# Issuing one pair's far-value loads behind the next pair's first query copies, in a hybrid decoder layer

## The chip, the cores and the metric

The kernel runs on one core of one Trainium2 chip. The metric is device time in microseconds (us) of one execution. The engines are TensorE (PE in the profile, with its weight loads as PEld), VectorE (DVE), ScalarE (ACT), GpSimd (POOL) and SyncE (SP), which here issues the DMAs (SPq in the profile).

## The reference

One decoder layer over 1024 tokens of width 1024. Two mixers share one input projection: an attention with 8 heads of 64 columns, and a gated recurrence with 4 heads of 128. Their outputs are joined and projected, then a squared-ReLU feed-forward of width 4096 follows; each part has an RMS norm ahead of it and one behind it. The change touches the attention alone:

```python
DILATED_PATTERNS = ((128, 1), (512, 4), (2048, 16))
...
def dilated_mixture_attention(q, k, v, slopes):
    outs, lses = [], []
    for window, dilation in DILATED_PATTERNS:
        o, lse = dilated_branch(q, k, v, slopes, window, dilation)
        outs.append(o)
        lses.append(lse)
    w = jax.nn.softmax(jnp.stack(lses, axis=0), axis=0)
    o = jnp.sum(w[..., None] * jnp.stack(outs, axis=0), axis=0)
    return o.astype(q.dtype)
```

Each pattern lets a query see keys at a stride (every key of the last 128, every 4th of the last 512, every 16th of all), with a bias that falls with the distance. Mixing the three by their denominators is the same as one softmax over the joint keys, with a bias table that counts how many patterns reach a key.

## The kernel before

**Numbers in two parts.** Every product is made in float32 by splitting each operand into a rounded part (names ending in h, or hi) and the rest (l, lo) and multiplying the parts (`three_pass`, lines 90 to 92: three matmuls).

**Stages.** The input is normed and turned, the recurrence's four heads run first (`hgrn_core`), and the attention's projections are laid between their steps. The attention then runs head by head, in four pairs of two heads; output projection and feed-forward follow.

**How the order is set.** The program is written out by hand. Projections are generators that hand out PE work in small pieces; `fill` takes pieces from them between the steps of the recurrence and of the attention, by estimated costs. Each engine works through its own list in program order, and so does SP: a DMA whose data are not ready, or whose target is still read, holds up all DMAs behind it. `attn_proj(pr)` projects pair `pr`: queries (`pm_aq`, in two halves of 512 tokens), values (`pm_av`) and keys (`pm_ak`). Pairs 0 and 1 are projected during the last recurrence head.

**Queries.** For each half, `qf` is written from PSUM by DVE (L793), ACT rounds it to `hiq` and POOL subtracts (`both_parts`, L719 and L720). Both tiles come from a pool of just two buffers with the tag "half", which the next half uses again. Four DMAs then copy the parts to the stacked query tiles `q` of the pair's two heads (L798 and L799). Those stacks come from the tag "S", whose nine buffers the recurrence's tiles use too: `q` of the second head of pair 1 takes the one that `at`, the score tile of the last recurrence head, held.

**Keys of pair 0.** `keys_read` writes the two parts of the keys and copies them with eight DMAs for each half (L737, names `hik`/`kf` for the first half and `kp` for the second).

**Values.** `values_turn` transposes the values of 512 tokens, writes them to `v`, and sends the blocks that the far keys need to a DRAM tile `vd` (L767). The far values are the keys beyond the near blocks, taken at stride 4. `far_load(pr)` takes two slabs and reads them back in far order: six DMAs at L672 into `vf`. For pair 0 it is called at the end of the second `values_turn`; for the other pairs from the attention's loop.

**The attention's steps.** For each head there are eight items: diagonal blocks D0 to D3, far F0 and F1, near N0 and N1. `look` multiplies keys and queries into a bank of the tag "s", of which there are two, and DVE adds the bias and takes the minimum (L901, tile `bt` holds the bias). `raise_` is ACT's exponential (L954), `turn` transposes on PE (`pt_D`, L964) and splits the result on ACT and DVE (`pth` L993, `ptl` L994), `weigh` multiplies with the values (`pov`, L1012, and `pov_far` with the far values, L1028). `swap_low` (L935, `px`) is a small product that moves minima between token orders; its bank is one of the two of "s" too. `gated` (L645) ends the last recurrence head on DVE.

Of the kernel before, what the change touches and what calls it, by code (L numbers as in the profile page):

```python
# [9 lines left out]
F32R = mybir.dt.float32r  # L10
# [7 lines left out]
P = 128  # L18
T = 1024
# [9 lines left out]
DIL = 4  # L29
# [3 lines left out]
def f32(ap):  # L33
    return ap.bitcast(F32)
# [3 lines left out]
def hymba_layer(ctx, tc, x, w_in, w_out, w_ff1, w_ff2, g_pre, lb_logits, g_mix, g_post,  # L38
# [13 lines left out]
    def slab(tag, name, dtype=F32, shape=(P, T)):  # L52
        return sp.tile(list(shape), dtype, tag=tag, name=name,
                       bufs={"S": 9, "T": 9, "P": 3, "BT": 2, "V8": 2, "R": 1}[tag])

    def bank(tag, name):
        return ps.tile([P, 512], F32, tag=tag, name=name,
                       bufs={"mm": 2, "s": 2, "t": 2, "pv": 2}[tag])

    def half(name, dtype=F32):  # L60
        return sp.tile([P, 512], dtype, tag="half", name=name, bufs=2)
# [86 lines left out]
    def w_get(i, ahead=1):  # L148
        while done[1] < min(i + 1 + ahead, len(stream)):
            w_split()  # L150
        return parts[i]
# [240 lines left out]
    def proj_t(w, name, hf, out_box):  # L392
        wh, wl = kc(w[0]), kc(w[1])
        pm = bank("mm", f"pm_{name}{hf}")
        for k in range(NK):
            three_pass(pm, (wh[:, k], wl[:, k]), part(hT, k, hf), k == 0, k == NK - 1)
            out_box[0] = pm
            if k < NK - 1:
                yield 650.0


    def in_blocks(ap):
        return ap.rearrange("p (j i r) -> p j r i", i=32, r=DIL)
# [4 lines left out]
    def by_class(ap):  # L408
        return ap.rearrange("p (j r i) -> p j r i", i=32, r=DIL)
# [58 lines left out]
    def rrow_by_class(hf):  # L468
        sl = slice(hf * 512, hf * 512 + 512)
        moved = half(f"rc{hf}")  # L470
        S.activation(moved.rearrange("p (r m) -> p r m", r=DIL), classes(rrow[:, sl]), AF.Copy)
        S.activation(rrow[:, sl], moved, AF.Copy)
# [187 lines left out]
    fars = {}  # L660

    def key_blocks(ap, j0, j1):
        return ap.rearrange("p (r j i) -> p j r i", r=DIL, i=32)[:, j0:j1]

    def far_load(pr):
        fars[pr] = [slab("T", f"vf{pr}_{c}", F32R, (P, DIL, 2, 2, 64)) for c in range(2)]
        v2 = v_dram[pr].rearrange("(two odd) k c -> odd k two c", odd=2)
        for c in range(2):
            for odd in range(2):
                for c_, p0, k0, n in ((0, 0, 64 * odd, P), (1, 0, P - P * odd, 64), (1, 64, P - P * odd, 64)):  # L670
                    if c_ == c:
                        nc.sync.dma_start(out=f32(fars[pr][c][p0:p0 + n]).rearrange(  # L672
                            "p (two odd) h a d -> odd p two (h a d)", odd=2)[odd], in_=v2[odd, k0:k0 + n])
# [42 lines left out]
    def both_parts(full, name, hi=None):  # L716
        eng = G if hi is None else V
        hi = half(f"hi{name}", F32R) if hi is None else hi
        S.activation(hi, f32(full), AF.Copy)  # L719
        eng.tensor_tensor(out=full, in0=f32(full), in1=f32(hi), op=ALU.subtract)  # L720
        return hi, full
# [34 lines left out]
    def values_turn(tag="mm"):  # L756
        pr, vs, full, hf = turn_later.pop(0)
        pt = bank(tag, f"pvt{pr}{hf}")
        for j in range(4):
            TE.transpose(pt[:, j * P:(j + 1) * P], full[:, j * P:(j + 1) * P], ident)  # L760
        ptv = pt.rearrange("p (j h d) -> p j h d", j=4, h=2)
        dst = vs[:, hf * 4:hf * 4 + 4]
        S.activation(dst[:, :, :, 0, :], ptv, AF.Copy)
        V.tensor_tensor(out=dst[:, :, :, 1, :], in0=ptv, in1=f32(dst[:, :, :, 0, :]), op=ALU.subtract)
        b = slice(0, 4) if hf == 0 else slice(4, 6)
        for r in range(DIL):
            nc.sync.dma_start(out=v_dram[pr][r].rearrange("(n i) c -> i n c", i=32)[:, b],  # L767
                              in_=f32(vs[32 * r:32 * r + 32, b]).rearrange("p n h a d -> p n (h a d)"))
        if hf == 1 and pr == 0:
            far_load(0)  # L770

    def attn_proj(pr):
        stacks = [{}, {}]
        box = [None]
        while pr > 1 and not second_done[pr - 2]:
            yield None
        w = w_get(A0 + 3 * pr, 0)
        for hf in range(2):
            sl = slice(hf * 512, hf * 512 + 512)
            for n, cost in enumerate(proj_t(w, f"aq{pr}", hf, box)):  # L780
                if hf == 0 and n == 3 and turn_later:
                    values_turn()
                    cost += 450.0
                if hf == 0 and n == 4:
                    w_get(A0 + 3 * pr)
                if pr == 0 and hf == 0 and n == 5:
                    rrow_by_class(1)
                yield cost
            if hf == 0:
                for i in range(2):  # L790
                    stacks[i]["q"] = slab("S", f"q{pr}_{i}", F32R)
            full = half(f"qf{pr}{hf}", F32R)
            V.tensor_tensor(out=by_class(f32(full)), in0=in_blocks(box[0]),  # L793
                            in1=rrow[:, sl].rearrange("p (r j i) -> p j r i", r=DIL, i=32), op=ALU.mult)
            hi, lo = both_parts(full, f"q{pr}{hf}")
            for i, (a, b) in enumerate(halves):
                c, d = halves[1 - i]
                nc.sync.dma_start(out=f32(stacks[i]["q"][a:b, sl]), in_=f32(hi[a:b]))  # L798
                nc.sync.dma_start(out=f32(stacks[i]["q"][c:d, sl]), in_=f32(lo[a:b]))  # L799
            yield 650.0  # L800
        wv = w_get(A0 + 3 * pr + 1, 0)
        vs = None

        def values(hf):
            for n, cost in enumerate(proj_t(wv, f"av{pr}", hf, box)):
                if n == 4 and (pr > 0 or hf == 0):
                    w_get(A0 + 3 * pr + 1 + hf)
                if pr == 0 and hf == 1 and n == 6:
                    values_turn("s")
                    cost += 450.0  # L810
                yield cost
            full = half(f"vf{pr}{hf}")
            V.tensor_tensor(out=by_class(full), in0=in_blocks(box[0]),
                            in1=rrow[:, hf * 512:hf * 512 + 512].rearrange("p (r j i) -> p j r i", r=DIL, i=32), op=ALU.mult)
            turn_later.append((pr, vs, full, hf))
            yield 650.0

        vs = slab("V8", f"v{pr}", F32R, (P, NT, 2, 2, 64))
        yield from values(0)
        if pr == 0:  # L820
            yield from values(1)
        while pr > 0 and not first_done[pr - 1]:
            yield None
        wk = w_get(A0 + 3 * pr + 2, 0)
        for i in range(2):
            stacks[i]["kh"] = slab("S", f"kh{pr}_{i}", F32R)
            stacks[i]["kl"] = slab("S", f"kl{pr}_{i}", F32R)
        pairs[pr] = (stacks, vs)
        for hf in range(2):
            for n, cost in enumerate(proj_t(wk, f"ak{pr}", hf, box)):  # L830
                if n == (3 if pr else 6) and hf == 0:
                    values_turn("mm" if pr else "s")
                    cost += 450.0
                if pr == 0 and hf == 1 and n == 5:
                    w_get(A0 + 2)
                yield cost
            keys_read(pr, box[0], hf)
            if hf == 0 and pr == AH // 2 - 1:
                early_rows()
            yield 650.0  # L840
        if pr > 0:
            yield from values(1)
# [273 lines left out]
    def early_rows():  # L1116


        early["rows"] = wide.tile([P, NE, AW], F32, tag="A", name="erows")
        early["table"] = wide.tile([P, 2, T], F32, tag="A", name="etable")  # L1120
        early["order"] = early["table"][:, 1, :P]
        G.tensor_copy(early["order"].rearrange("p (i r) -> p i r", r=DIL), ident.rearrange("p (r i) -> p i r", r=DIL))
        early["mt"] = [wide.tile([P, 2, 2, 4, P], F32R, tag="A", name=f"emt{q}") for q in range(NE // 2)]
        for q in range(NE // 2):
            nc.sync.dma_start(out=early["rows"][:, 2 * q:2 * q + 2],
                              in_=mix_dram[2 * q * P:2 * (q + 1) * P, :AW].rearrange("(n p) d -> p n d", p=P))
# [1180 lines left out]
```

## Time and profile before

| what | value |
|---|---|
| three runs | 1196.8, 1198.42, 1199.7 us (median 1198.42) |
| the profiled execution | 1198.21 us |
| its span, first to last instruction | 1196.4 us |
| mean granted TensorE clock | 0.997 |
| PE busy | 1183.7 us (99%) |
| DVE, ACT, POOL busy | 839.9, 548.6, 296.0 us |
| DMA queue that SP feeds | 174.37 MB, 45.2% of 16 engines' span |

The profile is one execution. Busy time of PE is modelled and counts a matmul as busy while it is in the pipeline, so neighbouring rows overlap. A row of a timeline has its start, its length, the engine, the source line, the operation, the tiles (written <- read) and in brackets the idle time of that engine just before it and what ended it. A row of the windows has the stretch, its length, the busy time of PE, PEld, DVE, ACT and POOL with the number of instructions, the granted clock of TensorE (1.00 is full), the share of the DMA engines in use and GB/s. A row of the waits says who waited for whom, the sum in us, how often, and the longest. SPq rows show the time in which SP issues a DMA, not the transfer.

### The profile page before, as it was taken

To read this page: it belongs to the slowest core of one execution; us is meant where nothing else is said; L and a number is where in the kernel's file an instruction comes from. 1 tells how busy PE (TensorE), PEld (TensorE's weight loads), DVE (VectorE), ACT (ScalarE), POOL (GpSimd) and SP (SyncE) were. 2 spreads that over 40 slices of the span, in tenths; PEclk is the share of its full clock that TensorE was granted. 3 is DMA by queue.
4 is the path that set the end of the run, shared out by engine and by line. 5 is a ranking of instruction groups with operands and counts; after the bars stand their busy time and mean duration, and the time that the engine had idled before them with its cause. 6 is when DMAs were issued, how large, how long until landed. Compare 5 with 4: busy or idle time off the path is not lost.

```text
span 1196.4 us, 17598 instructions
## 1 busy us (share of the span) xinstructions
PE 1183.7 (99%) x6486; PEld 1008.3 (84%) x6486; DVE 839.9 (70%) x1427; ACT 548.6 (46%) x1082; POOL 296.0 (25%) x283
## 2 busy tenths in 40 slices
PE   9999999999999999999999999999999999999997
PEld 8898989878888888888888888888888888888886
DVE  5686969586666667675697666766677653578796
ACT  7633424333556667755653222222244544444562
POOL 0121212001111110152512776566540000000022
PEclk9999999999999999999999999999999999999999
DMA  5222323137454555372424565553687434533337
GB/s 219 71 68 85 98 84 110 42 104 188 95 134 104 142 145 143 93 236 91 173 98 159 175 215 208 178 182 143 218 324 271 162 104 143 174 90 104 107 105 281
DMA packets 90549, 175.49 MB, mean 147 GB/s; under 512 B 14944, under 2 KB 42464, under 8 KB 90464
## 3 DMA queue, kind: packets, MB, share of 16 engines
q1 hardware_dynamic: 90320, 174.37, 45.2%
q8 instruction: 51, 0.84, 0.3%
q14 instruction: 34, 0.28, 0.1%
q10 hardware_dynamic: 144, 0.00, 0.0%
HBM read 116.91 MB, written 47.99 MB: 138 GB/s over the span
## 4 chain that ended last, share of the span: by engine, by line
PE 75%; ACT 1%; DMA 1%; DVE 1%; issue 0%; SPq 0%; DVEq 0%; POOLq 0%; POOL 0%; ACTq 0%
PE f L2047 18%; PE f2s L2047 7%; PE pwo L92 2%; PE pwo L90 2%; PE pwo L91 2%; PE pm_ak L90 1%; PE pm_ak L92 1%; PE pm_ak L91 1%; PE pm_aq L90 1%; PE pov L1012 1%; PE pm_aq L92 1%; PE pm_av L90 1%; PE pm_aq L91 1%; PE pm_av L92 1%; PE pm_av L91 1%; PE pt_D L964 1%
## 5 line engine op out<-in xcount | busy, mean ns | idle before, releaser
L87 DVE TENSOR_TENSOR al<-ar,ah 128x1024 fp32r<-128x1024 f32 x56 | 70.7, 1262 | 81.3 <-ACT ah L86 78.9
L2047 PE MATMUL f<-bh,ah 128*128 128x512 f32 x320 | 124.5, 389 | 0.0
L2047 PE MATMUL f<-bl,ah 128*128 128x512 f32 x320 | 124.5, 389 | 0.0
L2047 PE MATMUL f<-bh,al 128*128 128x512 f32 x320 | 124.5, 389 | 0.0
L86 ACT ACTIVATE ah<-ar 128x1024 fp32r<-128x1024 f32 x56 | 59.2, 1056 | 85.8 <-DMA ar<-actd 84.0
L2047 PEld LDWEIGHTS f<-bh,ah 128*128 128x128 f32 x320 | 60.1, 188 | 12.6
L2047 PEld LDWEIGHTS f<-bl,ah 128*128 128x128 f32 x320 | 60.1, 188 | 12.5
L2047 PEld LDWEIGHTS f<-bh,al 128*128 128x128 f32 x320 | 60.1, 188 | 12.3
L2121 POOL TENSOR_SCALAR lbl<-ssq 128x1 f32<-128x1 f32 x4 | 4.1, 1013 | 244.1 <-ACT fd L2117 243.8
L1670 POOL TENSOR_TENSOR e<-x,e 128x512 f32<-128x512 f32 x14 | 21.6, 1540 | 131.9 <-DVE x L1621 124.7
L2047 PE MATMUL f2s<-bh,al 128*128 128x512 f32 (+1 forms) x128 | 48.9, 382 | 0.0
L2047 PE MATMUL f2s<-bl,ah 128*128 128x512 f32 (+1 forms) x128 | 48.9, 382 | 0.0
L2047 PE MATMUL f2s<-bh,ah 128*128 128x512 f32 (+1 forms) x128 | 48.9, 382 | 0.0
L703 POOL TENSOR_SCALAR tout<-traw 128x256 f32<-128x256 f32 x16 | 18.3, 1146 | 101.0 <-DMA traw<-in_bias_tab_dram 101.0
L87 DVE TENSOR_TENSOR bl<-br,bh 128x1024 fp32r<-128x1024 f32 x32 | 40.2, 1255 | 0.8 <-ACT bh L86 0.7
L2064 ACT ACTIVATE acc<-f 128x512 f32<-128x512 f32 x28 | 16.7, 598 | 49.2 <-PE f L2047 49.2
L751 POOL TENSOR_TENSOR kl<-kf,kh 64x512 fp32r<-64x512 f32 x12 | 16.2, 1350 | 79.2 <-ACT kh L750 79.2
L86 ACT ACTIVATE bh<-br 128x1024 fp32r<-128x1024 f32 x32 | 33.6, 1051 | 3.4 <-PE f L2047 2.3
L87 DVE TENSOR_TENSOR wl<-raw,wh 128x1024 fp32r<-128x1024 f32 x21 | 25.7, 1225 | 9.9 <-ACT wh L86 9.9
L90 PE MATMUL pwo<-woh,mt 128*128 128x512 f32 x80 | 32.2, 403 | 0.0
L92 PE MATMUL pwo<-woh,mt 128*128 128x512 f32 x80 | 31.3, 391 | 0.0
L91 PE MATMUL pwo<-wol,mt 128*128 128x512 f32 x80 | 31.2, 390 | 0.0
(1723 smaller groups left out, 3899.0 us busy)
## 6 DMA issues: line engine op xcount, KB each, us to landing
ar<-actd SPq DMA_DIRECT2D x56, 512.0 KB, 3.6
br<-in_w_ff_dram SPq DMA_DIRECT2D x16, 1024.0 KB, 5.9
raw<-in_w_in_dram SPq DMA_DIRECT2D x28, 512.0 KB, 3.9
w1r<-in_w_ff_dram SPq DMA_DIRECT2D x14, 1024.0 KB, 6.4
actd<-e SPq DMA_DIRECT2D x17, 768.0 KB, 4.2
actd<-e SPq DMA_DIRECT2D x11, 1024.0 KB, 4.1
xr<-in_x_dram SPq DMA_DIRECT2D x8, 512.0 KB, 8.1
raw<-in_w_out_dram SPq DMA_DIRECT2D x8, 512.0 KB, 3.9
```

The source lines that it names most:

```text
L86: S.activation(hi, src, AF.Copy)
L87: eng.tensor_tensor(out=lo, in0=src, in1=f32(hi), op=ALU.subtract)
L90: TE.matmul(dst, lhs[0], rhs[0], start=start, stop=False)
L91: TE.matmul(dst, lhs[0], rhs[1], start=False, stop=False)
L92: TE.matmul(dst, lhs[1], rhs[0], start=False, stop=stop)
L703: G.tensor_scalar(by_class(dst[:, part_ * w:(part_ + 1) * w]), in_blocks(raw[:, FAR * DIL:]), 8.0, None, op0=ALU.mult)
L751: G.tensor_tensor(out=kl[a:b], in0=src, in1=f32(kh[a:b]), op=ALU.subtract)
L964: TE.transpose(pt[:, j * P:(j + 1) * P], st["D"][b][:, j * P:(j + 1) * P], ident)
L1012: TE.matmul(po[:, c0:256], v_of(vs, j), pt[q][:, j, c0:], start=j == 0 and q == 0, stop=j == nj - 1 and q == 1)
L1670: eng[0].tensor_tensor(out=e1[:, 3], in0=a21, in1=e1[:, 2], op=ALU.add)
L2047: TE.matmul(pm, a[:, j, c], b[:, j, d], start=start and j == 0 and q == 0, stop=stop and j == 1 and q == 2, skip_group_check=True)
L2064: S.activation(acc_at(p, i), pm, AF.Copy)
```

## The change

`far_load` is cut in two: `far_room` takes the slabs, `far_load` issues the six DMAs and takes the slabs only where that has not been done. For pair 0 the slabs are taken where they were, at the end of the second `values_turn`; the DMAs are issued in `attn_proj(1)`, behind the four copies of its first query half. The other pairs are as before.

```diff
+    def far_room(pr):
+        fars[pr] = [slab("T", f"vf{pr}_{c}", F32R, (P, DIL, 2, 2, 64)) for c in range(2)]
+
     def far_load(pr):
-        fars[pr] = [slab("T", f"vf{pr}_{c}", F32R, (P, DIL, 2, 2, 64)) for c in range(2)]
+        if pr not in fars:
+            far_room(pr)
...
         if hf == 1 and pr == 0:
-            far_load(0)
+            far_room(0)
...
                 nc.sync.dma_start(out=f32(stacks[i]["q"][c:d, sl]), in_=f32(lo[a:b]))
+            if pr == 1 and hf == 0:
+                far_load(0)
             yield 650.0
```

PE, DVE, ACT and POOL have the same instructions in the same order in both kernels; only SP's list changes. Its first place is behind the copies of pair 0's values to DRAM (`vd`): `vf` are the far values, `kh`, `kl` the stacked keys, `hik`, `kf` and `kp` their sources, `raw` a block of weights. Before:

```order
L767 DMA vd_634<-v_2880 32x4x256 x4
L767 DMA vd_634<-v_2880 32x2x256 x4
L672 DMA vf_0_3065<-vd_634 128x2x256 x2
L672 DMA vf_1_3066<-vd_634 64x2x256 x4
L737 DMA kh_0_3001<-hik_3078 64x4x128 x2
L737 DMA kh_1_3003<-hik_3078 64x4x128 x2
L737 DMA kl_0_3002<-kf_3076 64x4x128 x2
L737 DMA kl_1_3004<-kf_3076 64x4x128 x2
```

At the same place now:

```order
L771 DMA vd_634<-v_2880 32x4x256 x4
L771 DMA vd_634<-v_2880 32x2x256 x4
L741 DMA kh_0_3001<-hik_3072 64x4x128 x2
L741 DMA kh_1_3003<-hik_3072 64x4x128 x2
L741 DMA kl_0_3002<-kf_3070 64x4x128 x2
L741 DMA kl_1_3004<-kf_3070 64x4x128 x2
L107 DMA raw_3128<-in_w_in_dram 128x1024
```

The two groups of `vf` (six DMAs) are gone from here, and the keys follow the values directly. The second place is ten rows on, at pair 1's query copies: `q_0` and `q_1` are the stacks of its two heads, `hiq` and `qf` the two parts, `bt` the bias table of head 1. Before:

```order
L107 DMA raw_3187<-in_w_in_dram 128x1024
L798 DMA q_0_3215<-hiq_3219 64x512
L799 DMA q_0_3215<-qf_3217 64x512
L798 DMA q_1_3216<-hiq_3219 64x512
L799 DMA q_1_3216<-qf_3217 64x512
L855 DMA bt_3263<-tabd_639 128x704
L798 DMA q_0_3215<-hiq_3327 64x512
```

At the same place now:

```order
L107 DMA raw_3181<-in_w_in_dram 128x1024
L802 DMA q_0_3209<-hiq_3213 64x512
L803 DMA q_0_3209<-qf_3211 64x512
L802 DMA q_1_3210<-hiq_3213 64x512
L803 DMA q_1_3210<-qf_3211 64x512
L676 DMA vf_0_3065<-vd_634 128x2x256 x2
L676 DMA vf_1_3066<-vd_634 64x2x256 x4
L861 DMA bt_3263<-tabd_639 128x704
L802 DMA q_0_3209<-hiq_3327 64x512
```

The far loads now stand between the last copy of the first query half and the bias table; the copies of the second query half (`hiq_3327`) come behind both. Line numbers of the changed kernel are 4 to 6 higher here.

## The prediction

> **What bounds the kernel now.** I read the page first, then the waits of TensorE (PE), then the timelines of PE, VectorE (DVE), ScalarE (ACT) and the DMA queue (SPq) around the only place where PE stops for long, and last the windows of that place for the granted clock. The page:
>
> ```profile
> span 1196.4 us, 17598 instructions
> PE 1183.7 (99%) x6486; PEld 1008.3 (84%) x6486; DVE 839.9 (70%) x1427; ACT 548.6 (46%) x1082; POOL 296.0 (25%) x283
> ```
>
> PE is busy 1183.7 of 1196.4 us. A change that leaves PE's work alone can only give back idle PE time or a lowered clock. The longest waits of PE in the whole span (us in total, times, longest):
>
> ```profile
> PE ps_F L896 <- DVE stat L901: 1.7, 1, 1.7
> PE ps_D L896 <- DVE stat L901: 0.7, 1, 0.7
> PE px L935 <- DVE stat L901: 0.5, 1, 0.5
> ```
>
> The first and third lie at one place. PE's timeline there (start, us, what, then the idle time before it):
>
> ```profile
> 299.35 0.39 PE L92 MATMUL pm_av<-hTh,wl 128*128 128x512 f32 x1
> 300.19 0.38 PE L935 MATMUL px<-pick,swap 128*128 128x4 f32 x2 [0.45 <-DVE stat L901]
> 302.23 0.53 PE L896 MATMUL ps_F<-kh,qc 128*128 128x192 f32 x1 [1.66 <-DVE stat L901]
> ...
> 305.11 0.41 PE L1012 MATMUL pov<-pth,v 128*128 128x256 f32 x1
> ```
>
> So 0.45 + 1.66 = 2.11 us are idle. The windows of the next microseconds show a second loss (the number after POOL's is PEclk, the granted clock):
>
> ```profile
> 302.00:303.00 1.00, 0.77 (x4) 0.78 (x4) 0.69 (x4) 0.00 (x0) 0.00 (x0) 0.57 0.28 66
> 303.00:304.00 1.00, 1.00 (x6) 1.00 (x6) 0.57 (x4) 0.00 (x0) 0.00 (x0) 0.50 0.88 199
> 304.00:305.00 1.00, 1.00 (x4) 0.81 (x3) 0.84 (x5) 0.49 (x1) 0.00 (x0) 0.50 0.57 133
> 305.00:306.00 1.00, 1.00 (x6) 0.87 (x6) 0.67 (x3) 0.00 (x0) 0.00 (x0) 0.73 0.00 0
> ```
>
> Right behind the stop the clock is half, for about 3.4 us. What is lost is 0.43 + 0.50 + 0.50 + 0.27 = 1.70 us. One stop thus costs 2.11 + 1.70 = 3.81 us, 0.3% of the span. Who makes PE wait is in DVE's and ACT's timelines:
>
> ```profile
> 296.90 0.60 DVE L645 SCALAR_TENSOR_TENSOR gate<-po,hrs,gate 128x128 f32<-128x128 f32 x2
> 298.83 0.69 DVE L793 TENSOR_TENSOR qf<-pm_aq,rrow 128x512 f32<-128x512 f32 x1 [1.33 <-DMA q<-hiq]
> 299.44 0.68 DVE L901 CUSTOM_DVE_ANT_0 pd<-ps_D,bt 128x512 f32<-128x512 f32 x1
> 300.05 0.08 DVE L901 DVE_READ_ACCUMULATOR2_ANT stat<- 128x1 f32 x1
> 301.13 0.42 DVE L994 TENSOR_TENSOR ptl<-pt_D,pth 128x256 fp32r<-128x256 f32 x1 [1.00 <-ACT pth L993]
> ...
> 302.09 0.08 DVE L901 DVE_READ_ACCUMULATOR2_ANT stat<- 128x1 f32 x1
> ```
>
> ```profile
> 287.00 0.63 ACT L719 ACTIVATE hiq<-qf 128x512 fp32r<-128x512 f32 x1 [5.41 <-DMA kl<-kf]
> ...
> 299.61 0.63 ACT L719 ACTIVATE hiq<-qf 128x512 fp32r<-128x512 f32 x1 [4.11 <-DVE qf L793]
> ...
> 300.74 0.36 ACT L993 ACTIVATE pth<-pt_D 128x256 fp32r<-128x256 f32 x1
> ```
>
> DVE is free at 296.90 + 0.60 = 297.50, but the second pair's second query half (qf, L793) overwrites one of only two "half" buffers, and a DMA still reads that buffer until the copies q<-hiq of the first query half have landed. Everything behind it in DVE's order stands still: the look at ps_D (L901) that frees the bank px needs, and, by way of ACT (hiq, an exponential, then pth) and ptl, the look at ps_F that ends at 302.17 and lets PE go on at 302.23. Those copies are late because of SP's queue:
>
> ```profile
> 275.31 4.44 SPq L672 DMA_DIRECT2D vf<-vd  x6
> ...
> 292.39 0.48 SPq L798 DMA_DIRECT2D q<-hiq  x1
> 292.96 0.55 SPq L799 DMA_DIRECT2D q<-qf  x1
> 293.60 0.55 SPq L798 DMA_DIRECT2D q<-hiq  x1
> 294.20 0.63 SPq L799 DMA_DIRECT2D q<-qf  x1
> ...
> 300.26 0.46 SPq L798 DMA_DIRECT2D q<-hiq  x1
> ```
>
> From 275.31 to 294.83 SP issues almost without a pause, the six far loads first. The chain of waits shows the copy that ends last:
>
> ```profile
> 293.60 5.11 DMA q<-hiq
> ```
>
> 293.60 + 5.11 = 298.71, and DVE starts at 298.83.
>
> **The change part by part.** Nothing is added or removed. PE, DVE, ACT and POOL keep their order; the six far loads go from ahead of the first pair's key copies to behind the four copies of the second pair's first query half, ahead of the bias table bt. The room is still taken at the old place, so no buffer changes.
>
> What comes earlier: the sixteen key copies and two weight loads (raw) in between, by the 4.44 us of the far loads at most. SP would reach the first q<-hiq at 292.39 - 4.44 = 287.95. Its data come from these two rows, the second of them on GpSimd (POOL):
>
> ```profile
> 285.84 0.69 DVE L793 TENSOR_TENSOR qf<-pm_aq,rrow 128x512 f32<-128x512 f32 x1 [0.15 <-PE pm_aq L92]
> 287.76 1.29 POOL L720 TENSOR_TENSOR qf<-qf,hiq 128x512 fp32r<-128x512 f32 x1 [11.68 <-ACT hiq L719]
> ```
>
> The qf waits for PE and does not move. ACT's hiq at 287.00 waited for the key copies; it can now start at 286.53, so hiq is ready near 287.2 and POOL's part near 288.6. The third copy has a wait of its own. The tile q of the second head takes the buffer of the recurrence's score tile `at`, which this last pair of L629 matmuls still reads:
>
> ```profile
> 290.56 0.39 PE L629 MATMUL po<-inat,at 128*128 128x128 f32 x2
> ```
>
> It ends at about 290.95, so this copy goes out near 291.0, not at 293.60 - 4.44 = 289.16: it gains 2.6 us, not 4.4, and SP waits here with the far loads queued behind. With 5.11 us to landing, its own row of before, it lands at 296.1. That is 1.4 us before DVE is free at 297.50. So qf starts at 297.50, 298.83 - 297.50 = **1.33 us** earlier. The fourth copy goes out near 291.6 and lands near 296.7, before ACT needs its buffer for hiq at 299.61 - 1.33 = 298.28.
>
> What is late next: the chain behind qf is unchanged, so ps_F starts at 302.23 - 1.33 = 300.90. The ps_D look ends at 300.13 - 1.33 = 298.80, before PE gets to px, so px's wait of 0.45 goes, and of the 2.11 idle 0.78 stay, all in front of ps_F.
>
> The clock: idle 0.78 where it was 2.11. The nearest row on the other side is the 0.7 us wait of ps_D in the list of PE's waits; it lies in this window, whose clock is 1.00:
>
> ```profile
> 453.00:454.00 1.00, 0.26 (x2) 0.16 (x2) 1.00 (x4) 0.65 (x2) 0.00 (x0) 1.00 0.73 164
> ```
>
> I take the row it is nearest to: no drop, **1.70 us**. The bounds are 0 (it drops all the same) and 1.70. The Trainium skill (TensorE: Matmul & The Clock Gate, Part 1) puts the fall to half clock behind at least one idle window of about 3.4 us that runs free of the program. Here 2.11 us of idling, broken by px, were enough, so the measurement decides against the full idle window; the 3.4 us at half clock agree with the window's length. By the page's rule alone the clock term would not hang on this stop and the sum would be 1.33.
>
> What moves later: the far loads go out from about 292.2 to 292.2 + 4.44 = 296.7. Their first use (all of the kernel's far products, from the first at 313.9):
>
> ```profile
> L1028 PE MATMUL pov_far<-ptFh,vf x64: 221/275/306, 313.9 to 497.9; 128*128 128x128 f32 x64
> ```
>
> With the 5.11 us of the q copy they land by about 301.5 and are read at 313.9 - 3.0 = 310.9: the cover is 9 us of projection and near and diagonal work on PE; without it each us late is a us of PE. The bias table goes out near 296.7, in place of straight behind the fourth copy, lands by 302 and is first read here, 3 us earlier in the new time:
>
> ```profile
> 316.40 0.29 DVE L901 CUSTOM_DVE_ANT_0 pd<-ps_D,bt 128x128 f32<-128x128 f32 x1 [0.25 <-PE ps_D L897]
> ```
>
> The copies of the second query half (300.26 - 1.33 = 298.93) find SP free since about 297.3. All this costs nothing.
>
> The sum: 1.33 + 1.70 = 3.03 us. Nothing later gives it back: from pov at 305.11 on, ACT, DVE and SP follow PE's own results, and PE has no wait between there and the 0.7 us in the window from 453. The profiled execution took 1198.21 us (span 1196.4 and 1.8 around it), 0.21 below the median of 1198.42, so 1195.2 from its own time and 1195.4 from the median: I say 1195.3. The ends of the parts: the whole stop goes, 3.81, 1194.5; only the idle goes, 1.33, 1197.0.
>
> **The rivals.** (1) The clock term is not gained: 0.78 us idle still lowers the clock, or the drop, which need not fall in every execution, was missing in some runs of before, whose three times differ by 2.9 us. For it: under work the trace has this one drop alone, and I have no row between 0.7 and 2.11 us of idling. Time 1198.3 - 1.33 = 1197.0. (2) The copies land no earlier: the DMA engines, not SP's issuing, hold them up. Against it: the far loads' bytes leave that backlog too. Or DVE's qf comes free but something else holds PE to 302.23. Time 1198.3. (3) Slower: the far values come too late for pov_far. PE takes its matmuls in order and would stop for all the time beyond 310.9. To lose the 3.03 and 2.4 more (0.2%), landing must slip to 310.9 + 5.4 = 316.3, some 15 us beyond the estimate; landing 7 us beyond that point would give 1202. Only SP blocked at the third copy, or at POOL's part of qf, could do it. The Trainium skill (DMA: Bandwidth & Descriptors, Rules for kernel authors) speaks for this rival: issue a DMA early and wait for it late. The change gives up 17 us of lead and keeps 9. That the change does not do what it says is excluded by the order of SP's queue.
>
> **How the numbers follow.** My forecast 0.70, (1) 0.19, (2) 0.07, (3) 0.04. The range holds the forecast, (1) and some tenths for the spread of the runs around either: 1194.0 to 1197.4; it leaves out (2), (3) and the tails. About 0.2% (2.4 us, below 1196.0) is what a measurement can tell from no change. My forecast lies only 0.7 beyond it, so I give about a tenth of its chance to "within": faster 0.62, within 0.34, slower 0.04.
>
> **What would show it.** Right: qf L793 near 297.5 without a DMA wait; px without a wait; ps_F near 300.9 with a wait of about 0.8; a granted clock of 1.00 from 300 to 306; the third copy near 291.0; far loads from about 292 to 297; pov near 302.4 and pov_far near 310.9, without a wait. Wrong: the clock at half after the shorter stop (rival 1), a DMA still ahead of qf (rival 2), a PE wait for the far values (rival 3), or a new wait between 305 and 453.

## The result, and the profile after

| | before | changed |
|---|---|---|
| median of 15 runs each | 1198.42 us | 1195.46 us |
| lowest to highest | 1196.8 to 1200.2 | 1195.06 to 1195.93 |
| ratio to before, 95% interval | | 0.9976 [0.9968, 0.9984] |
| span of the profiled execution | 1196.4 | 1193.2 |

By the medians the changed kernel is 2.96 us faster, 0.24% by the ratio. The runs also lie closer together: 0.9 us apart where they were 3.4 apart.

The page of the changed kernel: PE's busy time is 1.5 us less with the same 6486 matmuls, since matmuls at half clock had been longer, and the rest of the 3.2 us is idle time.

```profile
span 1193.2 us, 17595 instructions
PE 1182.2 (99%) x6486; PEld 1007.7 (84%) x6486; DVE 840.0 (70%) x1427; ACT 548.8 (46%) x1082; POOL 295.0 (25%) x283
```

PE's waits of the changed kernel. (Lines are 4 to 6 higher than before: L902 was L896, L907 was L901.) The first row is the start of the span, ahead of PE's first product. The wait of px is gone, that of ps_F is 1.0 in place of 1.7:

```profile
PE pig L311 <- DVE zero L231: 1.0, 1, 1.0
PE ps_F L902 <- DVE stat L907: 1.0, 1, 1.0
PE ps_D L902 <- DVE stat L907: 0.7, 1, 0.7
```

PE's timeline at the place, px and ps_F, then pov and the first far product; it shows no wait at either of the last two:

```profile
299.42 0.28 PE L941 MATMUL px<-pick,swap 128*128 128x4 f32 x2
300.65 0.36 PE L902 MATMUL ps_F<-kh,qc 128*128 128x192 f32 x1 [0.95 <-DVE stat L907]
...
302.21 0.28 PE L1018 MATMUL pov<-pth,v 128*128 128x256 f32 x1
...
310.79 0.31 PE L1034 MATMUL pov_far<-ptFh,vf 128*128 128x128 f32 x1
```

The windows behind the stop have the full clock (1.00 behind POOL's count), and PE is busy all the time:

```profile
302.00:303.00 1.00, 1.00 (x8) 0.91 (x7) 0.97 (x6) 0.33 (x2) 0.00 (x0) 1.00 0.95 213
303.00:304.00 1.00, 1.00 (x10) 0.92 (x9) 0.41 (x2) 1.00 (x2) 0.00 (x0) 1.00 0.07 16
304.00:305.00 1.00, 1.00 (x7) 0.82 (x6) 0.75 (x1) 0.98 (x4) 0.00 (x0) 1.00 0.00 0
```

DVE runs qf straight behind the gate, without a DMA wait; the wait that remains is one for ACT's pth:

```profile
296.75 0.60 DVE L645 SCALAR_TENSOR_TENSOR gate<-po,hrs,gate 128x128 f32<-128x128 f32 x2
297.27 0.68 DVE L797 TENSOR_TENSOR qf<-pm_aq,rrow 128x512 f32<-128x512 f32 x1
...
299.56 0.42 DVE L1000 TENSOR_TENSOR ptl<-pt_D,pth 128x256 fp32r<-128x256 f32 x1 [1.01 <-ACT pth L999]
```

SP's queue has the key copies first, then the query copies, the third with a gap ahead of it, then the far loads and the bias table:

```profile
275.40 2.63 SPq L741 DMA_DIRECT2D kh<-hik  x4
...
287.71 0.48 SPq L802 DMA_DIRECT2D q<-hiq  x1
288.48 0.48 SPq L803 DMA_DIRECT2D q<-qf  x1
290.81 0.46 SPq L802 DMA_DIRECT2D q<-hiq  x1
291.33 0.59 SPq L803 DMA_DIRECT2D q<-qf  x1
291.97 4.79 SPq L676 DMA_DIRECT2D vf<-vd  x6
296.80 0.59 SPq L861 DMA_DIRECT2D bt<-tabd  x1
298.69 0.50 SPq L802 DMA_DIRECT2D q<-hiq  x1
```

The gap ahead of the third copy ends with the last product that reads the score tile (`at`), at 290.40 + 0.39 = 290.79:

```profile
290.40 0.39 PE L629 MATMUL po<-inat,at 128*128 128x128 f32 x2
```

### The profile page after: what moved, and what is told of

It reads as the page before. It is cut to its first block, busy times and chain, and to the rows that moved or that the text cites. A ratio compares the mean times of both kernels' runs of the same rounds, so it can differ in the third digit from the quotient of the medians.

```text
span 1193.2 us, 17595 instructions
## 1 busy us (share of the span) xinstructions
PE 1182.2 (99%) x6486; PEld 1007.7 (84%) x6486; DVE 840.0 (70%) x1427; ACT 548.8 (46%) x1082; POOL 295.0 (25%) x283
## 4 chain that ended last, share of the span: by engine, by line
PE 91%; DVE 4%; ACT 3%; issue 2%; POOL 0%; DMA 0%; DVEq 0%; POOLq 0%; ACTq 0%
PE f L2053 18%; PE f2s L2053 7%; PE pig L90 2%; PE pig L92 2%; PE pig L91 2%; PE pwo L92 2%; PE pwo L90 2%; PE pwo L91 2%; PE pm_ak L90 1%; PE pl L535 1%; PE pm_ak L92 1%; PE pm_ak L91 1%; PE pm_q L90 1%; PE pm_aq L90 1%; PE pm_q L91 1%
```

## The experiments

The theory: the far loads hold up the query copies in SP's queue; the copies still read the buffer that qf writes; what stands behind qf on DVE and ACT stops PE; and the stop lowers the clock. The chief rival: the loads cost by their bytes, in a stretch in which the DMA engines are full (their share was 1.06 from 290 to 295 in the kernel before), whoever waits for which buffer. A second: the clock falls for another cause.

**1. Another buffer, the loads left alone.** On the kernel before, the second query half of pair 1 gets a buffer of its own, and POOL still does the subtraction:

```diff
-    def both_parts(full, name, hi=None):
-        eng = G if hi is None else V
+    def both_parts(full, name, hi=None, eng=None):
+        eng = eng or (G if hi is None else V)
...
-            full = half(f"qf{pr}{hf}", F32R)
+            apart = slab("P", f"qp{pr}", F32R, (P, 2, 512)) if pr == 1 and hf == 1 else None
+            full = half(f"qf{pr}{hf}", F32R) if apart is None else apart[:, 0]
...
-            hi, lo = both_parts(full, f"q{pr}{hf}")
+            hi, lo = both_parts(full, f"q{pr}{hf}", None if apart is None else apart[:, 1], G)
```

> Kernel before with the far loads left where they were; only the second pair's second query half (qf and hiq) is written to another buffer, whose last readers are the first pair's key copies. Theory (qf waits for a buffer that the query copies still read, PE waits for what stands behind qf, and the clock falls behind that stop): qf starts at 297.5, ps_F at 300.9, no half clock, 1195.4 us, as with the change. Rival (the far loads cost because their bytes fill the DMA engines there, whoever waits for which buffer): the loads have not moved, so no gain, 1198.4 us.

Measured 1195.24 us (1194.9 to 1195.8 in 12 runs) against 1197.84 of before in the same session, ratio 0.9976 [0.9967, 0.9985]. Its rows of SP, DVE and PE:

```profile
275.19 4.45 SPq L672 DMA_DIRECT2D vf<-vd  x6
...
293.08 0.55 SPq L799 DMA_DIRECT2D q<-hiq  x1
```

```profile
297.02 0.68 DVE L794 TENSOR_TENSOR qp<-pm_aq,rrow 128x512 f32<-128x512 f32 x1
```

```profile
300.36 0.36 PE L897 MATMUL ps_F<-kh,qc 128*128 128x192 f32 x1 [0.91 <-DVE stat L902]
```

The far loads go out as early as before and the query copies nearly as late: the third goes out at 293.08 and takes 5.5 us to land, so it is still under way when qf starts at 297.02. The whole gain is there all the same. The rival of the bytes falls: the loads cost only through the buffer that qf waits for. What made the copies late, their late issue or the full DMA engines, this run does not separate.

**2. The gap filled.** On the kernel before, PE gets twelve products whose results nobody reads:

```diff
         TE.matmul(pS[:, :DIL], z, pick4, start=True, stop=True)
+        if hd == 0 and far == 0:
+            warm = part(hT, 0, 0)[0]
+            for _ in range(12):
+                TE.matmul(pS[:, 256:], warm[:, :P], warm[:, :256], start=True, stop=True, skip_group_check=True)
```

> Kernel before, and PE does twelve idle products of 128x256 (some 1.4 us, their result is not used) behind px, in the gap that ends at 302.23. Theory (the clock falls because PE idles for 2.1 us): the stop keeps its end at 302.23 but no half clock follows, 1.7 us gained, 1196.7 us. Rival (the half clock has another cause, or costs nothing): 1198.4 us, or 1199.8 if the products also delay ps_F.

Measured 1196.96 us (1196.07 to 1199.06) against 1197.84, ratio 0.9991 [0.9981, 1.0001]: half of what was expected, and the interval reaches no change. In its profiled execution the third query copy went out 0.83 us earlier than in the profile of before (292.77 against 293.60), qf ran at 298.30 in place of 298.83, and the products filled the rest:

```profile
299.64 0.39 PE L935 MATMUL px<-pick,swap 128*128 128x4 f32 x2
299.89 1.67 PE L939 MATMUL px<-hTh 128*128 128x256 f32 x12
301.69 0.36 PE L896 MATMUL ps_F<-kh,qc 128*128 128x192 f32 x1
```

```profile
302.00:303.00 1.00, 1.00 (x9) 0.93 (x8) 0.74 (x5) 0.25 (x1) 0.00 (x0) 1.00 0.69 162
```

ps_F still starts over a microsecond later than in the changed kernel, yet the clock stays at 1.00. But without the products the gap would have been 301.69 - 300.03 = 1.66 us here (px ends at 299.64 + 0.39), hardly more than the 1.56 us that lower no clock in experiment 7. So neither the time nor this one window settles much. The mean granted clock of each run speaks for the theory: it was 0.998 or 0.999 in all 12 runs here, and 0.997 or less in 12 of the 30 runs of before in the same session.

**3 and 7. DVE slowed down.** On the changed kernel, one more instruction ahead of qf (all of rrow in experiment 3, half of it in 7), which leaves rrow as it is:

```diff
+            if pr == 1 and hf == 1:
+                V.tensor_tensor(out=rrow, in0=rrow, in1=rrow, op=ALU.max)
             full = half(f"qf{pr}{hf}", F32R)
```

> Changed kernel with one more VectorE instruction of 128x1024 (1.25 us) straight ahead of the second query half's qf, nothing else moved. Theory (what counts is when qf runs, not where the far loads are): ps_F moves from 300.65 to about 301.9, 1.2 us lost by itself, and up to 1.7 us more by the clock, as PE idles about 1.9 to 2.2 us again: 1196.7 to 1198.4 us, the upper end likelier. Rival (the gain came from the DMA traffic): PE is hardly delayed, 1195.5 us.

> Changed kernel with one more VectorE instruction of 128x512 (0.69 us, some 0.6 in its pipeline) straight ahead of the second query half's qf. PE idles about 1.55 us ahead of ps_F where it was 0.95. Theory: 0.6 us lost by the delay, 1196.1 us; the clock falls in some executions at most, which would show as runs up to 1197.8. If the clock falls always at 1.55 us idle, 1197.8 us.

Experiment 3: 1198.19 us (1196.31 to 1199.94) against 1197.84, ratio 0.9997 [0.9986, 1.0007]: the gain is gone, with the loads in their new place. Stop and half clock are those of before:

```profile
300.02 0.39 PE L943 MATMUL px<-pick,swap 128*128 128x4 f32 x2 [0.34 <-DVE stat L909]
302.06 0.53 PE L904 MATMUL ps_F<-kh,qc 128*128 128x192 f32 x1 [1.65 <-DVE stat L909]
```

```profile
303.00:304.00 1.00, 1.00 (x6) 1.00 (x5) 0.69 (x5) 0.09 (x1) 0.00 (x0) 0.50 0.84 195
304.00:305.00 1.00, 1.00 (x4) 0.71 (x4) 0.87 (x4) 0.40 (x1) 0.00 (x0) 0.50 0.48 107
```

Its twelve runs lie in three groups: four at 1196.3 to 1196.9, six at 1197.9 to 1198.6, two at 1199.6 and 1199.9. The lowest fits the changed kernel plus the added idling alone (1195.46 + 1.99 - 0.95 = 1196.5), and the granted clock bears it out: it was 0.999 in these four runs and 0.997 or 0.998 in the eight others. Experiment 7: 1196.25 us (1195.77 to 1196.52 in 11 runs), ratio 0.9986 [0.9977, 0.9995], with one group only, a granted clock of 0.998 to 1.000 in all its runs, and this stop:

```profile
301.82 0.36 PE L904 MATMUL ps_F<-kh,qc 128*128 128x192 f32 x1 [1.56 <-DVE stat L909]
```

So 1.56 us of idling cost about their own length; 0.34 + 1.65 = 1.99 lowered the clock, in most executions but not in all, as the groups and their clocks say (one execution was profiled).

**4 and 8. ACT's order.** The rounding of the second query half is issued one step later, in 4 on the changed kernel, in 8 on the kernel before:

```diff
+            if pr == 1 and hf == 1:
+                yield 650.0
             hi, lo = both_parts(full, f"q{pr}{hf}")
...
-            yield 650.0
+            if pr != 1 or hf != 1:
+                yield 650.0
```

> Changed kernel; ScalarE's rounding of the second query half (hiq) is issued behind the exponential of D2 and the pth of D1, which now stand behind it and do not need it. Theory (the 0.95 us that PE still waits at ps_F come from ScalarE's order behind qf): ps_F at about 299.7, 0.9 us gained, 1194.5 us. Rival (the rest of the stop has another cause, or ScalarE's work is needed at the same time elsewhere): 1195.5 us.

> Kernel before (far loads at their old place) with ScalarE's rounding of the second query half issued behind the exponential of D2 and the pth of D1. The qf still waits until 298.8 for the query copies. Theory (the stop is the sum of the late qf and of ScalarE's order behind it): ps_F at about 301.2 in place of 302.23, PE idles about 1.1 us, no half clock, 1195.8 us. Rival (as long as the far loads stand ahead, the stop stays): 1198.4 us.

Experiment 4: 1194.30 us against 1197.84, ratio 0.9968 [0.9955, 0.9981]. ACT's pth no longer stands behind hiq, and PE goes from px to ps_F without a wait:

```profile
297.35 0.38 ACT L1002 ACTIVATE pth<-pt_D 128x256 fp32r<-128x256 f32 x1 [1.02 <-PE pt_D L973]
298.28 0.63 ACT L723 ACTIVATE hiq<-qf 128x512 fp32r<-128x512 f32 x1 [0.54 <-DVE qf L797]
```

```profile
299.68 0.28 PE L944 MATMUL px<-pick,swap 128*128 128x4 f32 x2
299.81 0.35 PE L905 MATMUL ps_F<-kh,qc 128*128 128x192 f32 x1
```

Experiment 8: 1195.41 us against 1198.19, ratio 0.9979 [0.9970, 0.9988]. DVE's qf waits for the copies as before, yet the stop is short and the clock does not fall:

```profile
298.81 0.69 DVE L793 TENSOR_TENSOR qf<-pm_aq,rrow 128x512 f32<-128x512 f32 x1 [0.93 <-DMA q<-qf]
```

```profile
301.11 0.36 PE L899 MATMUL ps_F<-kh,qc 128*128 128x192 f32 x1 [0.56 <-DVE stat L904]
```

Either half of the stop, the late qf or ACT's order behind it, can be taken away for nearly the same gain.

**5 and 6. The cover.** The far loads of the changed kernel are put off further: in 5 behind the second query half's copies, in 6 behind the recurrence's last output.

```diff
-            if pr == 1 and hf == 0:
+            if pr == 1 and hf == 1:
                 far_load(0)
```

```diff
-            if pr == 1 and hf == 0:
-                far_load(0)
...
-        3: lambda: last_gate(3),
+        3: lambda: [last_gate(3), far_load(0)],
```

> Changed kernel with the far loads put off once more, behind the four copies of the second query half: issued from about 301.9 to 306.4, landing by 309.5 to 311. First use at 310.8. Theory (cover is left as long as they land before 310.8): 1195.5 us, at most 0.3 more. Rival (a load put off is a load that is waited for): PE waits for the far values, over 1196 us.

> Changed kernel with the far loads behind the recurrence's last output (the DMA mixd at 307.07): issued from about 307.5 to 312, landing by 315. First use at 310.8. Theory (beyond 310.8 every us late is a us of PE, and a stop of over 2 us lowers the clock too): PE stops 4 us at the first far product, and 1.7 us more by the clock: 1199.5 to 1201.5 us. Rival (something else hides them): 1195.5 us.

Experiment 5: 1195.38 us against 1198.19, ratio 0.9981 [0.9972, 0.9989], as the changed kernel. The loads go out here, and the first far product has no wait for them:

```profile
301.67 3.77 SPq L676 DMA_DIRECT2D vf<-vd  x6
```

```profile
310.61 0.31 PE L1034 MATMUL pov_far<-ptFh,vf 128*128 128x128 f32 x1
```

Experiment 6: 1201.78 us (1201.38 to 1202.71) against 1198.19, ratio 1.0035 [1.0022, 1.0047]: 6.3 above the changed kernel's 1195.46, and just beyond the upper end of what was expected. Its SP, PE's two waits, and the windows:

```profile
307.31 4.34 SPq L676 DMA_DIRECT2D vf<-vd  x6
```

```profile
312.14 0.33 PE L1032 MATMUL pov_far<-ptFh,vf 128*128 128x128 f32 x1 [1.33 <-DMA vf<-vd]
314.37 0.66 PE L1032 MATMUL pov_far<-ptFh,vf 128*128 128x128 f32 x2 [1.79 <-DMA vf<-vd]
```

```profile
313.00:314.00 1.00, 0.00 (x0) 0.00 (x0) 0.00 (x0) 0.00 (x0) 0.00 (x0) 0.92 1.09 238
314.00:317.00 3.00, 2.63 (x8) 2.33 (x9) 0.00 (x0) 0.00 (x0) 0.00 (x0) 0.50 1.12 225
317.00:320.00 3.00, 3.00 (x11) 2.60 (x11) 0.30 (x2) 0.47 (x1) 0.00 (x0) 0.50 0.42 78
320.00:321.00 1.00, 1.00 (x7) 0.82 (x5) 0.69 (x1) 1.00 (x5) 0.00 (x0) 0.67 0.08 1
```

1.33 + 1.79 = 3.1 us idle, less than the 4 expected, but the half clock lasts twice as long as before: 0.08 + 1.50 + 1.50 + 0.33 = 3.4 us. Some 0.3 of these lie before 314.37, inside the wait itself, so 3.1 us of work are lost by the clock. With the 3.1 of waiting that is about 6.3, as the times say.

**9 to 11. What is best.** On one chip: the changed kernel unaltered (9), with the deferred rounding of experiment 4 (10), and the kernel before with both the buffer of experiment 1 and the deferred rounding, its loads in the old place (11; the edits are those above).

> The changed kernel once more, unaltered, so that the next two are compared with it on one chip: 1195.4 us.

> The changed kernel with the deferred rounding (hiq behind the exponential of D2 and the pth of D1) once more: 1194.3 us, 1.1 below the changed kernel on the same chip.

> Kernel before with the far loads at their old place, the second query half in another buffer and the deferred rounding. Theory (qf's buffer and ScalarE's order are all there is to the stop; where the far loads stand matters only through the buffer): no stop at ps_F and 1194.3 us, as with the changed kernel and the deferred rounding. Rival (moving the loads has a gain of its own): about 1195 us or more.

| | median | lowest to highest | ratio to before |
|---|---|---|---|
| 9 | 1195.43 | 1194.41 to 1195.76 | 0.9978 [0.9968, 0.9988] |
| 10 | 1194.44 | 1194.10 to 1195.00 | 0.9968 [0.9956, 0.9980] |
| 11 | 1194.43 | 1194.11 to 1194.88 | 0.9968 [0.9955, 0.9980] |

Before was 1198.09 in that session. PE has no wait at ps_F in 10 and 11; in 11 the row is this one:

```profile
299.95 0.34 PE L900 MATMUL ps_F<-kh,qc 128*128 128x192 f32 x1
```

Version 10 beats both kernels, by 1.0 us the changed one; 11 reaches the same without moving a load. In 11, too, the place of the loads is worth nothing by itself.

## Why the prediction was right

**The start of qf.** Forecast 297.50, found 297.27, without a DMA wait. DVE's gate ahead of it ran 0.15 us earlier in this execution (296.75 against 296.90), and qf's row starts 0.08 before the gate's ends. Experiment 1 shows that the buffer is the whole cause, experiment 3 that a late qf alone brings the loss back.

**What is late next.** ps_F was to start at 300.90 and started at 300.65. The idle time left was put at 0.78 and is 0.95. That px would no longer wait was in the sum. What was not: a px that does not wait starts before the row ahead of it ends (299.42 against 299.19 + 0.39 = 299.58) and is shorter (0.28 against 0.38). With the 0.16 by which PE's rows ran earlier in this execution, PE was through with px 0.42 us earlier than forecast (299.70 against 300.12), ps_F started only 0.25 earlier, and the difference is idle time. Its cause, ACT's order behind qf, is shown by experiment 4, which takes it away.

**The clock.** Forecast 1.00 from 300 to 306; found. The doubt was whether 0.78 us idle might still lower it; experiment 7 puts the margin at over 1.56. The prediction's list of the longest waits left out one row, that of `pig` with 1.0 us; it lies in the first 0.98 us of the span (granted clock 1.00), so it is no stop under work and changes nothing.

Rival 1 also had it that the drop need not fall in every execution of before. That was so. The two lowest of the 15 runs, at 1196.8, are 1.34 above 1195.46, which is the idle term without the clock term. In the three later sessions the kernel before ran 70 times: the mean granted clock was 0.999 in 24 of these runs (median 1196.9 us), 0.998 in 22, 0.997 in 17 (median 1198.3) and 0.996 in 7. (3.4 us at half clock take 1.70 / 1196 = 0.0014 off the mean of a run.) The changed kernel never had less than 0.998. The profiled execution of before was one with the drop (0.997), and its time lay near the median. That the sum of 1.33 + 1.70 = 3.03 came out at 2.96 is therefore luck in part: the sum holds for an execution with the drop, and the median need not be one. In the session in which both kernels ran again the gain was 1198.09 - 1195.43 = 2.66. The price of the clock term for one execution is read from the windows. The runs at 0.999 and 0.997 lie 1.4 us apart, near the 1.70, but their stops may have differed too, and no experiment took the clock term away by itself.

**The copies and the loads.** Third copy 291.0 forecast, 290.81 found, held by the score tile. Its way to landing was put at 5.11 us and took 3.3, so it landed near 294.1, not 296.1; as DVE is free only at 297.3, that changed nothing. Far loads 292.2 to 296.7 forecast, 291.97 to 296.76 found; bias table 296.7 and 296.80. pov at 302.4 and 302.21, the far product at 310.9 and 310.79, no wait for it. Rival 2 (the DMA engines hold the copies anyway, or something else holds PE) is excluded by qf's start without a wait and by ps_F at 300.65. Rival 3 was a matter of distance: experiment 5 issues the loads 9.7 us later still at no cost, experiment 6 pays. Its price was set too low in the prediction, which counted a us of PE for each us late: in experiment 6 the clock came on top, twice as long as in the kernel before.

## What to carry to other kernels

Where SP's queue is issued in order and is full, look for loads with much time to their first use ahead of copies that free a small pool's buffer; but ask first whether the wait is for the copy's data or for its source buffer, since another buffer gives the same without touching the queue. A late instruction on one engine costs by what stands behind it in the order of each engine: issue first what does not depend on it. Weigh a stop of PE with the windows behind it, since the lowered clock can cost nearly as much as the stop (1.70 beside 2.11 us here, 3.1 beside 3.1 in experiment 6).

## What the runs showed of the hardware that was not expected

The granted clock fell behind 1.99 and 2.11 us of idling, broken by a tiny product, but in none of 11 runs with 1.56. It did not fall in every run with the longer stops. A mean granted clock of 0.997 or less appears in 24 of the 70 runs of before in the later sessions, in 6 of 12 of experiment 3 and in all 5 of experiment 6, and in no run of the changed kernel or of the other experiments.

In experiment 3 the run times lie in steps, and the lowest step is the one at 0.999. A wide spread is not by itself a sign of the clock, though: experiment 2 had 0.998 or 0.999 in every run and spread over 3.0 us all the same, and the runs of before at 0.999 reach from 1196.0 to 1198.4. What spreads these was not tried.

The half clock lasted 3.4 us in the kernel before, and 6.8 us behind the 3.1 us of waiting in experiment 6. Why it was twice as long there was not tried. The longer stretch may occur in the kernel before too: the seven of the 70 runs with 0.996 are the slowest ones, all above 1200.1 us, and four of the five runs of experiment 6 have 0.996 as well. None of the seven was profiled.
